# Norm rows spread through DRAM instead of TensorE transposes, and key blocks in plain order

## The chip, the cores and the metric

The kernel runs on one core of a Trainium2 chip. A core has TensorE (PE: matrix products into PSUM), VectorE (DVE), ScalarE (ACT), GpSimd (POOL), SyncE (SP, which here only issues DMAs) and 16 DMA engines. Each engine works through its own instructions in order and waits on semaphores for the others. The metric is the device time of one execution in microseconds; before the change the median of three runs is 2652.79 (2652.48 to 2655.35).

## What is computed

A trunk of two layers over 2048 tokens of 1024 channels, in fp32. Cut to what matters here:

```
# layer A
h    = rms_norm(x, a_norm)
u, z = split(h @ w_in)
x    = x + ((pool(u) @ w_group * scale) * silu(z)) @ w_out
x    = x + (p[0] @ ple_w[0]) * sigmoid(x @ ple_gate_w[0])
# shared keys and values, from the stream after layer A
k, v = split(rms_norm(x, kv_norm) @ w_kv);   k = rms_norm(per head of k, k_norm)
# layer B
q, z = split(rms_norm(x, b_norm) @ w_in);    q = rms_norm(per head of q, b_q_norm)
o    = stick_breaking_attention(q, k, v)     # strictly causal, 16 heads of 64
x    = x + (o * silu(z)) @ w_out
x    = x + (p[1] @ ple_w[1]) * sigmoid(x @ ple_gate_w[1])
```

`rms_norm` multiplies each token by one number, 1/sqrt(mean of its squares + eps), and each channel by a gain. The gains are folded into the weights. The token numbers are multiplied in after the product: `(x @ w)` of a token times that token's number.

## The kernel before

**Layout.** Activations lie channel by channel: a tile has 128 channels as partitions and 512 tokens along its free dimension. The 2048 tokens are four chunks (`s`) of 512. Every fp32 operand of a product is split into a high and a low part, and a product is three matmuls of 128x512 (high by high, high by low, low by high).

**The first part** (lines 212 to 885) is a list of 22 steps per chunk: for each group g in 3, 2, 1, 0 a gate product `run_z` and a `run_u`; four `run_o`; four `run_g`; then `run_kvq` twice each for q, k and v. A gate or u product is 48 matmuls of 512 columns (two outputs, eight `kt`, three matmuls). A `run_kvq` step has two halves, token pairs `j0` = 0 and 2, each 48 matmuls over eight weight units (`kt`, six matmuls per unit). The weights of a step are fetched two steps ahead and converted (split into parts, with the gain) one step ahead: for the wide weights of q, k and v the first four units at the start of the step before, the other four in its middle (`mid`, line 855). The conversion of q, k, v weights is L148 on ACT and L149 on VectorE. Weights that come back in later chunks are stored converted and only reread (`reread`, line 111).

**What orders the work.** `keep_in_program_order` pins an instruction to its place in its engine's order; the others are placed by the compiler's scheduler. DMAs go through `queue` (line 88), which issues on SyncE and pins them in this part. `pend` (line 86) is a list of stores that `stored_late` (line 95) issues at the third weight unit of the next product; `late` is a list of finishing pieces that `settle` (line 265) runs after the next gate product or v half.

**Token norms of layer A.** `prep(s)` makes the norms of the chunk's tokens, `r`, a tile of 128 x 4: token `j*128 + t` is at partition t, column j. Products lie with tokens along the free dimension, so `r` is needed as a row of 512 tokens, equal on all 128 partitions. `bcast` (line 237) does that: four TensorE transposes of `r[:, j]` spread over 128 columns (L241) into PSUM, and an ACT copy to `rb` (L246). It is called after the first gate product (g = 3) of a chunk (line 482; for chunk 0 later, in `run_u`). `gate_of` then multiplies the gate product by `rb` (L490), and `run_u` the u product (L508). PSUM for these products is six banks (four and two), two per product.

**Token norms of layer B.** In the first q step the norms after layer A, `r2s[s]`, are made in the same way, 128 x 4 (line 634). Here the tokens are in another order: token `4*t + j` is at partition t, column j. The gate branch of layer B, `gate_z(c)` (line 1060), runs beside the attention, for chunks 3, 2, 1, 0, piece by piece between the attention's own matmuls. It reads eight pairs `xz`, makes its own row `rb` with four transposes (L1069) into a bank that it borrows from the attention (`psar`, from `psl` at the start, from `psa` later, two banks each) and an ACT copy that orders the tokens (L1071), and multiplies each product by it (L1077).

**Keys.** `keyed` and `normed` take the products of q and k with tokens as partitions, evacuate them (`qs`, L721), make per-head norms (`sqq`, `ssq`, `rq`), multiply (L732) and transpose them in 32x32 blocks on VectorE (L734) into the tile `blocks`. For each of four 128-token tiles j the transpose writes every fourth element, so that `blocks` holds a head's tokens in the order (t j). When the fourth is written, `finish(m)` for four m goes to the list `lag`, which runs in the next step after its first 48 matmuls: a copy to the high part on ACT and a subtraction on VectorE for the low part (for k L743 and L744, 512 elements each; for q L747 and L748, with the gain), and a store to DRAM.

**The second part** (lines 888 to 1310) is the attention: 160 slots of one head, 512 queries and 512 keys, each with two score matmuls (L956, L957), a sigmoid (L960), a scan on VectorE (L968, L965), transposes (L981), a split (L984, L985) and two matmuls with the values (L993, L994). Between them go the pieces of the gate branch and of the output part (L1043, L1045, L1047), in shares worked out beforehand.

Of the kernel before, what the change touches and what calls it, by code (L numbers as in the profile page):

```python
# [9 lines left out]
F32 = mybir.dt.float32  # L10
F32R = mybir.dt.float32r
AF = mybir.ActivationFunctionType
ALU = mybir.AluOpType
AX = mybir.AxisListType

P = 128
D = 1024
S = 2048
KT = D // P
# [3 lines left out]
W5 = 512  # L23
NSUB = S // W5
# [6 lines left out]
def f(ap):  # L31
    return ap.bitcast(F32)
# [3 lines left out]
def trunk_kernel(ctx, tc, x, xt, pt0, wut, cols, heads, zin, grp, aout, agate, aple,  # L36
                 bq, kv, bz, bout, bgate, bple, outt):
    nc = tc.nc
# [28 lines left out]
    qd = [[[dram.tile([2, 4, P, P], F32, name=f"qd{i}{s}_{m}") for i in range(2)] for m in range(NH // 2)] for s in range(NSUB)]  # L67
    kd = [[dram.tile([2, 4, P, P], F32, name=f"kd{s}_{m}") for m in range(NH // 2)] for s in range(NSUB)]
    vd = [[dram.tile([8, W5, P], F32, name=f"vd{s}_{b}") for b in range(2)] for s in range(NSUB)]
    ve = [[dram.tile([4, W5], F32, name=f"ve{s}_{b}") for b in range(2)] for s in range(NSUB)]  # L70

    wod = [dram.tile([P, 2, 2, 4, P], F32, name=f"wod{o}") for o in range(KT)]
# [13 lines left out]
    pend = []  # L86
# [125 lines left out]
    with ExitStack() as st:  # L212
# [17 lines left out]
        hp = st.enter_context(tc.tile_pool(name="hp", bufs=1))  # L230
        work = hp.tile([P, 4, HALO + W5], F32, name="work")
        blocks = work.rearrange("q e n -> q (e n)")[:, 0 : 4 * W5].rearrange("q (g t j) -> q g t j", j=4, t=32)
        halo = [[hp.tile([P, HALO], F32, name=f"halo{o}_{i}") for i in range(2)] for o in range(KT)]
        for o in range(KT):
            V.memset(halo[o][0], 0.0)
# [231 lines left out]
        def run_z(s, g, wz):  # L467
            ck = chunk[s]
            beside = ()
            if not s and g == 3:  # L470
                beside = first_beside()
                wz = wz0["pair"]
            elif not s and g:
                beside = turning(g - 1)
            pss2 = [dense(), dense()]
            product(pss2, wz, ck["x"], (0, P), range(KT), beside)
            settle()
            if not s and g == 3:
                ck["z3"] = pss2
                return  # L480
            if "rb" not in ck:
                ck["rb"] = bcast(ck["r"], "x")
            gate_of(ck, g, pss2)

        def gate_of(ck, g, pss2):
# [122 lines left out]
        def run_kvq(s, kind, b, ws):  # L608
            ck = chunk[s]
            for j0 in (0, 2):  # L610
                if j0 and state["mid"]:
                    state.pop("mid")()
                    state["mid"] = None
                pss2 = [dense(), dense()]
                for kt in range(KT):
                    for i in range(2):
                        tk = slice((j0 + i) * P, (j0 + i + 1) * P)
                        for xh, wh in ((0, 0), (1, 0), (0, 1)):
                            T.matmul(pss2[i], ck["x2"][kt][:, xh, tk], wst(ws, kt, wh, 0, W5),  # L619
                                     start=(kt == 0 and xh == 0 and wh == 0), stop=(kt == KT - 1 and wh == 1))  # L620
                    if kt == 2:
                        stored_late()
                    while j0 == 0 and kt == KT - 1 and lag:
                        lag.pop(0)()
                    if kind != "q" and kt == 4 and s + 1 < NSUB:
                        next(ck["nxt"], None)
                if "r2" not in ck:
                    ps = turned()
                    for j in range(4):
                        T.matmul(ps[:, 0, j : j + 1], ck["acc"][:, j * P : (j + 1) * P], ones,  # L630
                                 start=True, stop=True)
                    ss = t2.tile([P, 4], F32, tag="ssx", name="ss2")
                    A.copy(out=ss, in_=ps[:, 0, 0:4])
                    rsqrt_mean(r2s[s], ss, D, t2, "x")
                    ck["r2"] = r2s[s]
                fins = [fin for i in range(2) for fin in token_major(s, kind, b, j0 + i, pss2[i])]
                if kind == "v":
                    settle()
                    (early["v"] if s == NSUB - 1 and b else late).extend(fins)
                else:  # L640
                    for fin in fins:
                        fin()
                quarter = {("q", 1): 0, ("k", 0): 1, ("k", 1): 2, ("v", 0): 3}.get((kind, b))
                if quarter is not None and j0 == 0 and s + 1 < NSUB:
                    load_x(s + 1, quarter)
                    load_tokens(s + 1, quarter)
                    if "nxt" not in ck:
                        ck["nxt"] = prep(s + 1)
            if kind == "v" and b == 1 and s + 1 < NSUB:
                for _ in ck["nxt"]:  # L650
                    pass
# [78 lines left out]
        def normed(s, kind, b, j, qs, rq):  # L730
            tc.keep_in_program_order(
                V.tensor_tensor(out=qs, in0=qs, in1=rq.unsqueeze(2).to_broadcast([P, 8, HD]), op=ALU.mult))  # L732
            tc.keep_in_program_order(
                V.transpose(out=blocks[:, :, :, j], in_=qs.rearrange("q h (g t) -> q (h g) t", t=32)))  # L734
            if j < 3:
                return

            def finish(m):
                hl = t2.tile([P, 2, 2, 2, P], F32R, tag="t4", name="hl", bufs=4)
                src = blocks[:, 4 * m : 4 * m + 4].rearrange("q (e g) t j -> q e g (t j)", e=2)  # L740
                hi, lo = hl[:, :, 0], hl[:, :, 1]
                if kind == "k":
                    A.copy(out=hi, in_=src)  # L743
                    V.tensor_tensor(out=lo, in0=src, in1=f(hi), op=ALU.subtract)  # L744
                else:
                    for g in range(2):
                        A.activation(out=hi[:, :, g], in_=src[:, :, g], func=AF.Identity, scale=gqk[:, g : g + 1])  # L747
                        V.scalar_tensor_tensor(out=lo[:, :, g], in0=src[:, :, g], scalar=gqk[:, g : g + 1],  # L748
                                               in1=f(hi[:, :, g]), op0=ALU.mult, op1=ALU.subtract)

                def store():
                    whole = f(hl).rearrange("q e l g n -> q e (l g n)")
                    if kind == "k":
                        queue(out=kd[s][4 * b + m].rearrange("e a (p x) n -> (a p) e (x n)", x=4), in_=whole)
                        return
                    qa, qb = qd[s][4 * b + m]
                    queue(out=qa.rearrange("e a (p x) n -> (a p) e (x n)", x=4), in_=whole)
                    for l in range(2):
                        queue(out=qb.rearrange("e a (p l g) n -> l (a p) e (g n)", l=2, g=2)[l],
                              in_=f(hl)[:, :, 1 - l].rearrange("q e g n -> q e (g n)"))  # L760

                pend.append(store)

            for m in range(4):
                lag.append(lambda m=m: finish(m))
# [122 lines left out]
    with ExitStack() as st:  # L888
# [171 lines left out]
        def gate_z(c):  # L1060

            xs = chunk[c]["x2"] if c == NSUB - 1 else []
            for o in range(len(xs), KT):
                pr = pair("xz")
                nc.sync.dma_start(out=f(pr), in_=x2p[c][o])
                xs.append(pr)
            ps = (psl if "w" in early else psa).tile([P, 4, P], F32, tag="psl" if "w" in early else "psa", name="psar")
            for j in range(4):
                T.transpose(ps[:, j, :], r2s[c][:, j : j + 1].to_broadcast([P, P]), ident)  # L1069
            rb = kap.tile([P, W5], F32, tag="rb", name="rb")  # L1070
            A.copy(out=rb.rearrange("q (t j) -> q t j", j=4), in_=ps.rearrange("q j t -> q t j"))  # L1071
            for o in range(KT):
                wz = early.pop("w") if "w" in early else stored(wzd[o])
                ps = dense()
                yield from piecewise(ps, wz, xs, 0)
                zr = t2.tile([P, W5], F32, tag="tmp", name="zr", bufs=4)
                V.tensor_tensor(out=zr.rearrange("q (t j) -> q t j", j=4), in0=ps.rearrange("q (j t) -> q t j", j=4),  # L1077
                                in1=rb.rearrange("q (t j) -> q t j", j=4), op=ALU.mult)

                def silu(o=o, zr=zr):  # L1080
                    sg = t2.tile([P, W5], F32, tag="tmp", name="sgz", bufs=4)
                    stay(A.activation(out=sg, in_=zr, func=AF.Sigmoid))  # L1082
                    G.tensor_tensor(out=zr, in0=zr, in1=sg, op=ALU.mult)  # L1083
                    nc.sync.dma_start(out=zd[c][o], in_=zr)

                soon(1, silu)
                if c == 0:
                    pair_up(NSUB - 1)
# [272 lines left out]
```

## Time and profile before

| what | value |
|---|---|
| median of three runs | 2652.79 us (2652.48 to 2655.35) |
| profiled execution | 2653.59 us, span of its instructions 2651.8 us |
| TensorE clock granted | 1.0 throughout |
| first part, until the last v product | to about 1305 us |
| VectorE busy in 1305 to 1720 us | 398.3 of 414.7 us |
| DMA | 600.40 MB, mean 226 GB/s |

A row of a timeline reads: start in us, duration in us, engine, source line, operation, tile written <- tiles read, partitions x elements, count of merged instructions, and in brackets the idle time of the engine before it and who ended that. `SPq` is SyncE's queue. A row by source line gives counts and the durations' minimum, median and maximum in ns. A row of waits gives who waited <- for whom, the total in us, the number of times and the longest. Of the chain of waits a row is start, duration, what. Matmuls overlap, so the duration of one (0.39 us) is longer than the distance from one to the next (0.227 us).

### The profile page before, as it was taken

The page shows a single profiled execution, that of the slowest core. Times are in us where ns is not written, and L with a number is a line of the kernel's source. Part 1 is how long each engine was busy: PE and PEld are TensorE (multiplying, and loading weights), DVE is VectorE, ACT ScalarE, POOL GpSimd, SP SyncE. Part 2 cuts the span into 40 slices and gives each one's busy share as a digit, 9 for nine tenths or more (in the row PEclk, how much of TensorE's full clock was granted, in tenths as well). Part 3 has the DMA queues.
Part 4 walks back from the last instruction along what each step waited for, and adds up shares of the span by engine and source line. Part 5 has one row for each costly group of instructions (what it writes and reads, how often), then busy time and mean ns, then how long its engine had stood idle before and what let it go on. Part 6 is the DMA issues. An engine that isn't in the chain of part 4 may idle for free.

```text
span 2651.8 us, 38568 instructions
## 1 busy us (share of the span) xinstructions
PE 2640.3 (100%) x13102; PEld 2205.3 (83%) x13102; DVE 1984.8 (75%) x2570; ACT 1427.5 (54%) x2767; POOL 939.8 (35%) x740
## 2 busy tenths in 40 slices
PE   9999999999999999999999999999999999999999
PEld 8888888888888888888888888888888888888887
DVE  6767835677367763767599999999999998886633
ACT  5446523556136641455466666666666666665531
POOL 2665437644485444753221111122111211212220
PEclk9999999999999999999999999999999999999999
DMA  8658885587856878447787665556766777779865
GB/s 325 227 165 302 283 314 186 191 300 253 308 177 225 301 237 304 147 153 240 229 277 229 187 215 170 175 164 194 209 200 173 190 217 238 201 209 287 248 229 178
DMA packets 469826, 600.40 MB, mean 226 GB/s; under 512 B 28607, under 2 KB 308415, under 8 KB 469629
## 3 DMA queue, kind: packets, MB, share of 16 engines
q1 hardware_dynamic: 463272, 587.39, 67.7%
q0 software_dynamic: 4608, 8.39, 2.0%
q10 hardware_dynamic: 1748, 2.17, 0.3%
q8 instruction: 103, 1.69, 0.3%
q14 instruction: 95, 0.77, 0.1%
HBM read 438.40 MB, written 153.16 MB: 223 GB/s over the span
## 4 chain that ended last, share of the span: by engine, by line
PE 89%; DMA 3%; DVE 2%; POOL 2%; ACT 2%; issue 1%; SPq 0%; ACTq 0%; DVEq 0%; POOLq 0%
PE psd L619 16%; PE psa L981 9%; PE psd L166 8%; PE psd L167 8%; PE psd L168 8%; PE psd L1043 6%; PE psd L1045 6%; PE psd L1047 6%; PE pso L994 5%; PE psl L957 5%; PE pso L993 5%; PE psl L956 5%; DMA wraw<-in_bq_dram 1%; PE psdt L1043 1%; PE psdt L1045 1%
## 5 line engine op out<-in xcount | busy, mean ns | idle before, releaser
L619 PE MATMUL psd<-wpair,x 128*128 128x512 f32 x2304 | 525.6, 390 | 1.4 <-DVE wpair L149 0.8
L968 DVE TENSOR_TENSOR_SCAN pp<-kap,pp,zeros 128x512 f32<-128x512 f32 x384 | 512.7, 1337 | 7.8 <-ACT kap L960 7.1
L984 ACT CAST at<-psa 128x512 fp32r<-128x512 f32 (+3 forms) x640 | 325.7, 523 | 348.8 <-PE psa L981 337.8
L619 PEld LDWEIGHTS psd<-wpair,x 128*128 128x128 f32 x2304 | 431.7, 188 | 93.0 <-DVE wpair L149 2.2
L985 DVE TENSOR_TENSOR at<-psa,at 128x512 fp32r<-128x512 f32 (+3 forms) x640 | 374.9, 598 | 62.2 <-ACT at L984 57.7
L960 ACT ACTIVATE kap<-psl 128x512 f32<-128x512 f32 (+3 forms) x640 | 345.7, 540 | 93.9 <-PE psl L957 90.4
L981 PE MATMUL psa<-ident,pp 128*128 128x128 f32 x2176 | 329.4, 273 | 2.3 <-DVE at L985 1.5
L981 PEld LDWEIGHTS psa<-ident,pp 128*128 128x128 f32 x2176 | 263.7, 141 | 58.4 <-DVE at L985 4.2
L956 PE MATMUL psl<-kk,qa 128*128 128x512 f32 (+3 forms) x640 | 275.1, 430 | 0.2 <-DMA kk<-kd 0.2
L965 DVE TENSOR_TENSOR_SCAN pp<-kap,ahead 128x128 f32<-128x128 f32 (+3 forms) x256 | 224.2, 877 | 40.2 <-ACT kap L960 38.8
L994 PE MATMUL pso<-at,vv 128*128 128x512 f32 (+3 forms) x640 | 234.0, 366 | 0.0
L957 PE MATMUL psl<-kk,qb 128*128 128x512 f32 (+3 forms) x640 | 232.9, 364 | 0.0
L993 PE MATMUL pso<-at,vv 128*128 128x512 f32 (+3 forms) x640 | 232.2, 363 | 0.0
L167 PE MATMUL psd<-xp,wpair 128*128 128x512 f32 x512 | 199.5, 390 | 1.4 <-DVE xp L320 1.4
L166 PE MATMUL psd<-xp,wpair 128*128 128x512 f32 x512 | 200.1, 391 | 0.7 <-ACT xp L319 0.7
L168 PE MATMUL psd<-xp,wpair 128*128 128x512 f32 x512 | 199.3, 390 | 0.0
L149 DVE SCALAR_TENSOR_TENSOR wpair<-wraw,gains,wpair 128x512 fp32r<-128x512 f32 x192 | 164.8, 891 | 31.9 <-ACT wpair L148 30.9
L143 POOL TENSOR_TENSOR wpair<-wraw,wpair 128x512 fp32r<-128x512 f32 x99 | 145.1, 1475 | 78.9 <-ACT wpair L141 72.2
L148 ACT ACTIVATE wpair<-wraw,gains 128x512 fp32r<-128x512 f32 x192 | 129.7, 716 | 47.4 <-DMA wraw<-in_bq_dram 35.6
L1083 POOL TENSOR_TENSOR zr<-zr,sgz 128x512 f32<-128x512 f32 x32 | 61.4, 1919 | 263.8 <-ACT sgz L1082 236.6
L141 ACT CAST wpair<-wraw 128x512 fp32r<-128x512 f32 x148 | 89.1, 618 | 104.5 <-PE psd L168 61.1
L994 PEld LDWEIGHTS pso<-at,vv 128*128 128x128 f32 x640 | 120.3, 188 | 26.4
(206 smaller groups left out, 5400.4 us busy)
## 6 DMA issues: line engine op xcount, KB each, us to landing
kk<-kd SPq DMA_DIRECT2D x160, 256.0 KB
vv<-vd SPq DMA_DIRECT2D x160, 256.0 KB
wraw<-in_kv_dram SPq DMA_DIRECT2D x128, 256.0 KB
wpair<-wzd SPq DMA_DIRECT2D x64, 512.0 KB
wpair<-wod SPq DMA_DIRECT2D x64, 512.0 KB
wpair<-wgd SPq DMA_DIRECT2D x64, 512.0 KB
wpair<-wu SPq DMA_DIRECT2D x48, 512.0 KB
wpair<-wi SPq DMA_DIRECT2D x36, 512.0 KB
```

The source lines that it names most:

```text
L166: T.matmul(ps, wst(units, kt, 0, c0), acts[kt][:, 0], start=(begin and kt == order[0]), stop=False)
L167: T.matmul(ps, wst(units, kt, 0, c0), acts[kt][:, 1], start=False, stop=False)
L168: T.matmul(ps, wst(units, kt, 1, c0), acts[kt][:, 0], start=False, stop=(end and kt == order[-1]))
L619: T.matmul(pss2[i], ck["x2"][kt][:, xh, tk], wst(ws, kt, wh, 0, W5), start=(kt == 0 and xh == 0 and wh == 0), stop=(kt == KT - 1 and wh == 1))
L956: T.matmul(ps[:, :w], qa[:, qs], kk[:, :w], start=True, stop=False)
L957: T.matmul(ps[:, :w], qb[:, qs], kk[:, :w], start=False, stop=True)
L960: A.activation(out=kp[:, r0:], in_=ps[:, :w], func=AF.Sigmoid, scale=-1.0)
L968: V.tensor_tensor_scan(out=pp[:, ::-1], data0=kp[:, ::-1], data1=zeros.to_broadcast([P, W5]), initial=st["carry"][j], op0=ALU.mult, op1=AL ...
L981: T.transpose(pt[:, j * P : (j + 1) * P], pp[:, r0 + kt * P : r0 + (kt + 1) * P], ident)
L985: V.tensor_tensor(out=at[:, 1, cs], in0=pt[:, cs], in1=f(at[:, 0, cs]), op=ALU.subtract)
L993: T.matmul(po[:, cs], vv[:, kt, :], at[:, 0, cs], start=(st["diag"] and kt == 0), stop=False)
L994: T.matmul(po[:, cs], vv[:, kt, :], at[:, 1, cs], start=False, stop=(st["last"] and kt == 3))
```

## The change

Three edits.

1. For chunks 1 to 3, `r` is no longer transposed. A store of `r` to a DRAM tile `rxd[s]` (token order, 512 pieces of four bytes) joins `pend` ahead of the first gate product, so it is issued at its third unit; at the seventh unit (`kt == 6`) a DMA reads the row back onto all 128 partitions (256 KB written). Both go through `queue`, pinned. Chunk 0 keeps `bcast`.
2. For the gate branch, `r2s[s]` is stored to `r2d[s]` through `pend` in the first q step, and `gate_z` reads it back by a DMA onto all partitions. Transposes, the borrowed bank and the ACT copy go, for all four chunks. `rb` there remains one buffer.
3. For keys the block transpose writes tokens in the order (j t), contiguous for each j; the finish reads them in the order (t j), in steps of 32 elements (128 bytes), and is cut in two pieces of 256 elements per m. Queries stay as they were.

```
+    rxd = [dram.tile([4, P], F32, name=f"rxd{s}") for s in range(NSUB)]
+    r2d = [dram.tile([P, 4], F32, name=f"r2d{s}") for s in range(NSUB)]
...
+        plain = work.rearrange("q e n -> q (e n)")[:, 0 : 4 * W5].rearrange("q (g j t) -> q g j t", j=4, t=32)
...
         def run_z(s, g, wz):
+            if s and g == 3:
+                pend.append(lambda: queue(out=rxd[s].rearrange("j t -> t j"), in_=ck["r"]))
+
+                def spread():
+                    ck["rb"] = t2.tile([P, W5], F32, tag="rb", name="rbx", bufs=1)
+                    queue(out=ck["rb"], in_=rxd[s].rearrange("j t -> (j t)").unsqueeze(0).to_broadcast([P, W5]))
+
+                def behind():
+                    for kt in range(KT):
+                        if kt == 6:
+                            spread()
+                        yield
+
+                beside = behind()
...
-            if "rb" not in ck:
-                ck["rb"] = bcast(ck["r"], "x")
             gate_of(ck, g, pss2)
...
                     ck["r2"] = r2s[s]
+                    pend.append(lambda: queue(out=r2d[s], in_=r2s[s]))
...
-                V.transpose(out=blocks[:, :, :, j], in_=qs.rearrange("q h (g t) -> q (h g) t", t=32)))
+                V.transpose(out=plain[:, :, j] if kind == "k" else blocks[:, :, :, j], in_=qs.rearrange("q h (g t) -> q (h g) t", t=32)))
...
                 if kind == "k":
-                    A.copy(out=hi, in_=src)
-                    V.tensor_tensor(out=lo, in0=src, in1=f(hi), op=ALU.subtract)
+                    at = plain[:, 4 * m : 4 * m + 4].rearrange("q (e g) j t -> q e g t j", e=2)
+                    for e in range(2):
+                        hi, lo = (hl[:, e, l].rearrange("q g (t j) -> q g t j", j=4) for l in range(2))
+                        A.copy(out=hi, in_=at[:, e])
+                        V.tensor_tensor(out=lo, in0=at[:, e], in1=f(hi), op=ALU.subtract)
...
-            ps = (psl if "w" in early else psa).tile([P, 4, P], F32, tag="psl" if "w" in early else "psa", name="psar")
-            for j in range(4):
-                T.transpose(ps[:, j, :], r2s[c][:, j : j + 1].to_broadcast([P, P]), ident)
             rb = kap.tile([P, W5], F32, tag="rb", name="rb")
-            A.copy(out=rb.rearrange("q (t j) -> q t j", j=4), in_=ps.rearrange("q j t -> q t j"))
+            nc.sync.dma_start(out=rb, in_=r2d[c].rearrange("t j -> (t j)").unsqueeze(0).to_broadcast([P, W5]))
```

## Prediction

> **What bounds the kernel now.** I read the page's totals first, then the waits of TensorE, the chain of waits, and the timelines of single stretches.
>
> ```profile
> span 2651.8 us, 38568 instructions
> PE 2640.3 (100%) x13102; PEld 2205.3 (83%) x13102; DVE 1984.8 (75%) x2570; ACT 1427.5 (54%) x2767; POOL 939.8 (35%) x740
> ...
> PE psd L619 <- DVE wpair L149: 0.8, 1, 0.8
> PE psa L981 <- ACT rb L1071: 0.7, 1, 0.7
> ...
> 232.91 120.25 PE psd L619 x528
> ...
> 550.33 119.80 PE psd L619 x528
> ```
>
> The span is TensorE: 2640.3 us busy of 2651.8. "Busy" alone would prove little, but the chain of waits shows 528 matmuls of 512 columns in 119.80 us, 0.227 each, without a hole. So time comes off only where TensorE loses work or one of its few waits, and goes on only where a new wait appears. Two waits lie at places the change touches: 0.8 us for converted weights (L149), 0.7 us for the spread norms of the gate branch (L1071). The profiled execution took 2653.59 us, 1.8 more than its span; the three timed runs have a median of 2652.79 (2652.48 to 2655.35). I work out differences on the span and add them to that median. What a measurement here can tell from no change is about 0.2%, 5.3 us.
>
> **The transposes that go.** Timeline of TensorE at the first gate product of chunk 1, and where the gate branch's second spread stands:
>
> ```profile
> 363.88 0.60 PE L241 MATMUL pst<-ident,rx 128*128 128x128 f32 x4
> 364.24 0.48 PE L166 MATMUL psd<-xp,wpair 128*128 128x512 f32 x1
> 364.55 0.39 PE L167 MATMUL psd<-xp,wpair 128*128 128x512 f32 x1
> ...
> 1422.22 0.40 PE L994 MATMUL pso<-at,vv 128*128 128x512 f32 x1
> 1423.30 0.66 PE L981 MATMUL psa<-ident,pp 128*128 128x128 f32 x4 [0.69 <-ACT rb L1071]
> ```
>
> From the start of the four transposes to the next matmul is 0.36 us, and that matmul takes 0.31 to the next instead of 0.227: 0.44 us per group. Chunks 1 to 3 lose one group each and the gate branch four: 7 x 0.44 = 3.1 us, all of it on the path, since nothing else ends last there. The gate branch's group also holds a bank of the attention's transposes until ACT has copied it: start to start is 1.08 us at 1422 instead of 0.23, so 0.85 more goes; with small remains elsewhere I take 1.0 (estimate). Together 4.1 us off. The ACT copies that go were off the path.
>
> **What takes their place on the queues.** Chunk 1, the SyncE queue and its neighbours, with the window from 364 to 375 us (last three columns: clock, DMA share, GB/s) and the nearest DMA whose landing is recorded; then the gate branch from chunk 3 to chunk 2:
>
> ```profile
> 333.82 1.01 POOL L81 TENSOR_TENSOR rx<-ms,neghalf 128x4 f32<-128x4 f32 x1
> ...
> 360.66 5.28 SPq L90 DMA_DIRECT2D wpair<-wi  x4
> 366.04 6.44 SPq L90 DMA_DIRECT2D vd<-vv  x3
> 372.57 3.29 SPq L90 DMA_DIRECT2D wpair<-wu  x4
> ...
> 374.75 1.37 DVE L508 TENSOR_TENSOR work<-psd,rbx 128x512 f32<-128x512 f32 x2 [8.32 <-PE psd L168]
> ...
> 364.00:375.00 11.00, 11.00 (x52) 9.15 (x51) 1.54 (x3) 1.81 (x3) 2.54 (x2) 1.00 1.03 375
> ...
> os<-ob POOLq DMA_DIRECT2D x16, 256.0 KB, 4.4
> ...
> 1421.63 0.65 DVE L1077 TENSOR_TENSOR zr<-psd,rb 128x512 f32<-128x512 f32 x1
> ...
> 1426.77 0.32 SPq L1084 DMA_DIRECT2D zd<-zr  x1
> ...
> 1442.79 0.67 DVE L1077 TENSOR_TENSOR zr<-psd,rb 128x512 f32<-128x512 f32 x1
> ```
>
> The norms are ready at 334.8 (rx), long before. The store is queued behind the wi loads and the vd stores behind the read, so SyncE issues the store at about 366, in the middle of a stretch where the DMA engines are full (share 1.03, 375 GB/s, so 512 KB take 1.4 us). The store waits out what is queued ahead, some four to six such transfers, 6 to 8 us. The read waits for the store's landing and needs a few us more: the nearest row is 4.4 us for 256 KB. That puts the norms at about 376 to 378, after the product's end at 363.9, not within it. VectorE waits for them in front of the gate's multiply; behind it on VectorE stand the u product's two L508, due at 374.75, which slip by some 3 us. TensorE does not feel it: a gate product's two PSUM banks are asked for again two products later, at about 386 (six banks, two per product, 10.9 us each). What SyncE delays is the three vd stores and then the weights of the product at 386. They were issued from 372.57; while the DMA engines still drain what is ahead, only the 3 us or so are lost in which they run dry. At most 8 transfers of 1.4 us ahead of them put them at 384 at the latest before, so 2 to 5 us of cover. I put this edit at nothing; if the cover went, each us beyond it would cost 1 us in each of three chunks.
>
> In the gate branch the read of the next chunk's row waits until the last multiply with the old one (1421.63 to 1422.28) is done. SyncE issued nothing until 1426.77, so the read fits in; by 4.4 us it lands near 1427, and the next multiply with it starts at 1442.79. Nothing, again. The token store of r2 is one small DMA behind stores that wait longer: nothing.
>
> **The keys' blocks.** This is the step that decides. What each operation costs now, by source line:
>
> ```profile
> L259 ACT CAST x<-tx x32: 1075/1108/1137, 180.8 to 1177.5; 128x512 fp32r<-128x512 f32 x32
> L260 DVE TENSOR_TENSOR x<-tx,x x32: 1073/1253/2103, 182.4 to 1178.6; 128x512 fp32r<-128x512 f32 x32
> L250 ACT CAST kpair<-kraw x40: 388/614/632, 143.9 to 1157.0; 128x512 fp32r<-128x512 f32 x32, 128x256 fp32r<-128x256 f32 x8
> L743 ACT CAST hl<-work x32: 613/617/623, 305.3 to 1276.5; 128x512 fp32r<-128x512 f32 x32
> L246 ACT COPY rbx<-pst x4: 587/587/587, 43.5 to 999.9; 128x512 f32<-128x512 f32 x4
> L1071 ACT COPY rb<-psar x4: 586/586/589, 1306.3 to 1717.2; 128x512 f32<-128x512 f32 x4
> L744 DVE TENSOR_TENSOR hl<-work,hl x32: 670/684/694, 305.9 to 1277.4; 128x512 fp32r<-128x512 f32 x32
> L734 DVE STREAM_TRANSPOSE work<-qs x64: 1080/1094/1122, 240.6 to 1273.8; 128x512 f32<-128x512 f32 x64
> ```
>
> The transpose now writes every fourth element, 1094 ns; contiguous, no row shows it. Its bounds are 684 (L744, 512 contiguous elements on the same engine) and 1094; I take 684, because L260 reads at the same 16-byte steps and takes 1073 at best. So 0.41 us less for each of 32. In return the finish reads steps of 128 bytes, in pieces of 256 elements, twice as many. A contiguous piece of 256 takes 388 ns on ACT (L250's least). For the step the nearest row is L259: reading at 16-byte steps takes 1108 against 617, 0.49 more for 512 elements, 0.245 for 256. So 388 to 635 ns; I take 635, because L259's step also leaves its neighbours behind each time. Between two in a row ACT overlaps 0.1 us: 0.53 each. VectorE's subtractions grow alike (L744's 684 towards L260's 1073 for 512 elements, in halves), beside ACT's casts and no later than they.
>
> [...]
>
> Now where this stands. The last transposes of one k step and the finish come just ahead of the conversions that the next step needs:
>
> ```profile
> 304.14 1.10 DVE L734 STREAM_TRANSPOSE work<-qs 128x512 f32<-128x512 f32 x1
> ...
> 305.27 1.67 ACT L743 CAST hl<-work 128x512 fp32r<-128x512 f32 x3 [9.50 <-DVE work L734]
> 306.85 0.61 ACT L319 CAST xp<-xin 128x512 fp32r<-128x512 f32 x1
> 307.37 0.61 ACT L743 CAST hl<-work 128x512 fp32r<-128x512 f32 x1
> 307.89 0.68 ACT L721 ACTIVATE qs<-psd,r2all 128x512 f32<-128x512 f32 x1
> ...
> 315.93 1.78 DVE L149 SCALAR_TENSOR_TENSOR wpair<-wraw,gains,wpair 128x512 fp32r<-128x512 f32 x1
> ...
> 335.24 4.43 DVE L149 SCALAR_TENSOR_TENSOR wpair<-wraw,gains,wpair 128x512 fp32r<-128x512 f32 x4 [1.63 <-ACT wpair L148]
> ...
> 632.28 0.75 DVE L149 SCALAR_TENSOR_TENSOR wpair<-wraw,gains,wpair 128x512 fp32r<-128x512 f32 x1
> ...
> 633.88 2.66 DVE L149 SCALAR_TENSOR_TENSOR wpair<-wraw,gains,wpair 128x512 fp32r<-128x512 f32 x4
> ...
> 951.85 14.53 PE L619 MATMUL psd<-wpair,x 128*128 128x512 f32 x62 [0.83 <-DVE wpair L149]
> ```
>
> ACT stands still 9.5 us for the transpose, then does the finish, and only then evacuates the next keys (qs), whose squares, norm and multiply stand ahead of the L149 conversions on VectorE. So ACT's finish shifts the whole chain: four casts at 0.52 become eight at 0.53, +2.2, and the transpose ends 0.41 earlier: +1.75 us. How much cover is there? The first v step begins seven half steps of 10.89 after the rows above: at 309.1 in chunk 0 and 626.6 in chunk 1. Its unit 6 is first needed 38 matmuls later (0.227 each), at 317.7 and 635.2, and is ready at 317.71 and about 634.55 (first of the four at 633.88); unit 5 in chunk 1 at 633.0 for 633.8. So the cover is nothing in chunk 0, 0.6 in chunk 1, and in chunk 2 TensorE waits already (0.83 at 951.85). Chunk 3 has no next chunk to prepare beside it; I put it at nothing. That makes 1.7 + 1.15 + 1.75 = 4.6 us. The second v step meets the next finish, with the first delay still in the chain: in chunk 0 its first late unit is ready not before 336 for 337, so some 0.9 us there, 0.5 in chunk 1, none in chunk 2, whose TensorE is itself later: 1.4 us. In all 6.0 us, with bounds of 0 (388 ns pieces) and well above.
>
> **Sum:** 4.1 off, 6.0 on: +1.9 us on the median, 2654.7.
>
> **The rivals.** *The steps cost ACT nothing.* Eight at 0.30 are 2.4 for 2.1, and the transpose pays that back: no new wait, -4.1, and with the 0.8 that TensorE waits today -4.9: 2647.9. For it: reads from PSUM in large steps are not dearer here (L1071 takes 586 ns as L246 takes 587). Against it: L259, L260 and L734, all in SBUF.
>
> *The 128-byte step costs more than the 16-byte one.* Slower, at the same place: each 0.1 us on a piece adds 0.8 us to the chain in three chunks, and again in the second v step. At 0.75 per piece the chain is 3.5 late: 3.45 + 2.9 + 3.5 in the first v steps and about 5.7 in the second, 15.5; less 4.1 is +11.4, 2664.2. It decides from about 0.62 per piece, where the sum passes 5.3. For it: nothing in the trace is as far apart; the cover is nil. Against it: each step leaves its neighbours already at 16 bytes.
>
> *The store is slow.* 512 pieces of four bytes may take far longer than the queue ahead. From some 4 us over my 6 to 8, weights come late in three chunks; 4 us beyond that cover gives +12 and 2667. For it: no row has such a store. Against: it moves 2 KB. [...]
>
> *It isn't what it says:* attention may be paced by VectorE, so that the gate branch's transposes give nothing: +1.8 worse, 2656.5, inside the forecast's own range. Against it: one matmul follows the other there too.
>
> **How the numbers follow.** Forecast 0.55 (2651 to 2658), no cost of steps 0.20, dearer steps 0.19, slow store 0.06. Faster by over 5.3 us needs the whole first rival and a little luck: 0.08 of its 0.20, and 0.02 from elsewhere, 0.10. Slower: most of the dearer steps (0.16), of the slow store (0.05) and 0.04 of the forecast's upper end, 0.25. Same: 0.65. The range reaches from 2647.2, just beyond the first rival's time, to 2661.0, into the dearer steps at about 0.68 per piece; it leaves out 0.06 below and 0.14 above.
>
> **What would show it.** Right: TensorE has 28 matmuls fewer; waits of TensorE for L149 grow to about 6 us in chunks 0 to 2, none in chunk 3; the finish's casts take about 635 ns and the keys' transposes about 684; VectorE's first gate multiply in chunks 1 to 3 starts some 11 us later without a wait of TensorE. Wrong: casts near 388 ns, transposes still at 1094, or TensorE waiting for weights in the gate products or for rb in attention.

## The result, and the profile after

The changed kernel takes 2673.14 us (median of six runs, 2671.99 to 2675.75); the kernel before took 2654.17 in six runs beside it (2652.48 to 2655.35). The ratio is 1.0074 (95% interval 1.0061 to 1.0087): slower by some 19 us. The forecast was 2654.7 with a range up to 2661.0; the measured time lies beyond it. The profiled execution took 2673.71 us; its span is 20.0 us longer than before.

The totals on the page of the profile, as quoted of before:

```profile
span 2671.8 us, 38591 instructions
...
PE 2644.3 (99%) x13074; PEld 2207.6 (83%) x13074; DVE 1993.2 (75%) x2602; ACT 1445.3 (54%) x2792; POOL 939.4 (35%) x740
```

TensorE has the 28 instructions fewer, and is yet busy 4.0 us longer; the other 16 us are waits. TensorE's waits (who <- for whom, total, times, longest):

```profile
PE psd L168 <- DMA wpair<-wu: 10.6, 3, 4.0
PE psd L634 <- DVE wpair L151: 6.2, 4, 2.3
...
PE pst L645 <- POOL acc L619: 0.6, 1, 0.6
```

The second row is the keys' edit: the converted weights that cost 0.8 us before (L149 there, L151 here). The first is new: three times, once in each of chunks 1 to 3, the second u product of the chunk waits for its weights from DRAM. SyncE's queue in chunk 1 shows why:

```profile
363.68 4.53 SPq L92 DMA_DIRECT2D wpair<-wi  x3
368.30 0.39 SPq L92 DMA_DIRECT2D rxd<-rx  x1
379.82 0.32 SPq L92 DMA_DIRECT2D rbx<-rxd  x1
380.23 4.14 SPq L92 DMA_DIRECT2D vd<-vv  x3
384.46 2.68 SPq L92 DMA_DIRECT2D wpair<-wu  x1
```

Store issued at 368.30, read issued at 379.82, when the store had landed: 11.5 us in which SyncE issues nothing. The windows of the same stretch (the last two columns are DMA share and GB/s) show the DMA engines running dry:

```profile
372.00:374.00 2.00, 2.00 (x10) 1.66 (x9) 0.00 (x0) 0.00 (x0) 0.00 (x0) 1.00 0.96 349
374.00:376.00 2.00, 2.00 (x11) 1.65 (x10) 0.00 (x0) 0.00 (x0) 0.00 (x0) 1.00 0.07 11
376.00:378.00 2.00, 2.00 (x11) 1.65 (x10) 0.00 (x0) 0.00 (x0) 0.00 (x0) 1.00 0.00 0
...
380.00:382.00 2.00, 2.00 (x10) 1.66 (x9) 0.00 (x0) 0.00 (x0) 0.00 (x0) 1.00 0.00 0
382.00:384.00 2.00, 2.00 (x10) 1.68 (x9) 0.00 (x0) 0.00 (x0) 0.00 (x0) 1.00 0.85 190
```

The queue ahead is done by about 374.6, and then nothing moves for 7 us. The weights behind are issued 11.9 us later than before (384.46 against 372.57). VectorE's first gate multiply, and then TensorE at the second u product:

```profile
384.49 0.69 DVE L505 TENSOR_TENSOR zr<-psd,rbx 128x512 f32<-128x512 f32 x1 [20.21 <-DMA rbx<-rxd]
...
387.90 0.39 PE L170 MATMUL psd<-xp,wpair 128*128 128x512 f32 x1
391.64 0.75 PE L168 MATMUL psd<-xp,wpair 128*128 128x512 f32 x1 [3.36 <-DMA wpair<-wu]
392.19 0.63 PE L169 MATMUL psd<-xp,wpair 128*128 128x512 f32 x1
392.62 0.63 PE L170 MATMUL psd<-xp,wpair 128*128 128x512 f32 x1
```

Besides the wait there is a second cost: behind it the matmuls start 0.43 us apart in place of 0.227. The windows on either side (after PEld, DVE, ACT, POOL comes the granted clock):

```profile
384.83:388.25 3.42, 3.42 (x16) 2.52 (x14) 3.42 (x5) 1.27 (x2) 2.30 (x3) 1.00 1.13 330
388.25:391.66 3.41, 0.05 (x2) 0.05 (x1) 0.60 (x2) 0.00 (x0) 3.41 (x5) 1.00 1.00 370
391.66:395.07 3.41, 3.41 (x8) 2.76 (x9) 2.21 (x4) 0.62 (x1) 1.98 (x4) 0.50 1.03 418
395.07:398.48 3.41, 3.41 (x16) 2.79 (x16) 2.44 (x3) 0.00 (x0) 2.15 (x2) 1.00 1.02 413
```

For 3.41 us the granted clock is 0.50: 8 matmuls instead of 16, 1.7 us lost. This happens five times in after, never before: behind the three waits for wu and behind the two longest waits of the keys (at 320.0 and 968.5 us). In two of the five windows TensorE stands for a part, and less is lost: it is busy 3.41, 3.41, 2.91, 3.13 and 3.41 us in them, 16.3 in all, and half of that is the loss.

The ledger on the span: transposes and the borrowed bank 4.1 off (forecast); waits for wu 10.6 on; waits for converted weights 6.2 less 0.8, 5.4 on; half clock 8.1 on; GpSimd's `acc` 0.6 on. That is 20.6 against 20.0 measured.

### The profile page after: what moved, and what is told of

Same layout as the page of the kernel before. It is cut to its first block, busy times and chain, and to the rows that moved or that the text cites. A ratio compares the mean times of both kernels' runs of the same rounds, so it can differ in the third digit from the quotient of the medians.

```text
span 2671.8 us, 38591 instructions
## 1 busy us (share of the span) xinstructions
PE 2644.3 (99%) x13074; PEld 2207.6 (83%) x13074; DVE 1993.2 (75%) x2602; ACT 1445.3 (54%) x2792; POOL 939.4 (35%) x740
## 4 chain that ended last, share of the span: by engine, by line
PE 81%; POOL 5%; DMA 4%; DVE 4%; ACT 3%; issue 3%; SPq 0%; ACTq 0%; DVEq 0%; POOLq 0%
PE psa L1000 9%; PE psd L634 8%; PE psd L168 8%; PE psd L169 7%; PE psd L170 7%; PE psd L1062 6%; PE psd L1064 6%; PE psd L1066 6%; PE pso L1013 5%; PE psl L976 5%; PE pso L1012 5%; PE psl L975 5%; POOL rq L83 2%; DVE wpair L151 1%; DMA wraw<-in_bq_dram 1%
## 5 line engine op out<-in xcount | busy, mean ns | idle before, releaser
L168 PE MATMUL psd<-xp,wpair 128*128 128x512 f32 x512 | 201.8, 395 | 11.8 <-DMA wpair<-wu 10.6
L151 DVE SCALAR_TENSOR_TENSOR wpair<-wraw,gains,wpair 128x512 fp32r<-128x512 f32 x192 | 166.1, 897 | 33.3 <-ACT wpair L150 33.3
```

The lines of the kernel that those rows point to most:

```text
L168: T.matmul(ps, wst(units, kt, 0, c0), acts[kt][:, 0], start=(begin and kt == order[0]), stop=False)
```

## The experiments

The theory after this reading: edit 1 costs the time, because its store of 512 four-byte pieces lands late and SyncE stands at the read with the weights behind it; edit 3 costs about what was forecast; edit 2 gains. The rival: it is the edits together, the row's wait biting only on a chain that the keys' blocks have made longer. All ratios are to the kernel before, timed beside it on the same chip.

### Each edit alone

**`only_row`: edit 1 alone.**

```
+            if s and g == 3:
+                pend.append(lambda: queue(out=rxd[s].rearrange("j t -> t j"), in_=ck["r"]))
...
-            if "rb" not in ck:
-                ck["rb"] = bcast(ck["r"], "x")
```

> Only the first edit: the row of layer A's norms stored at the third unit of the first gate product and read back at the seventh; gate branch and keys as before. Theory (the store's landing holds SyncE, so the weights of the third product after it come late, and TensorE then runs some us at half clock): SyncE waits about 11 us between store and read in chunks 1 to 3, TensorE waits 3 to 4 us for weights there, each followed by 3.4 us at clock 0.5; about 16 us on, 1.3 us off for the transposes, so 2669 us. Rival (the late weights need the delays of the keys' edit as well): TensorE waits under 1 us there, the time within 3 us of before.

Measured: 2669.73 us, ratio 1.0066 (1.0053 to 1.0080). TensorE's waits, with two others left out between:

```profile
PE psd L167 <- DMA wpair<-wu: 7.8, 2, 4.3
PE psd L167 <- DVE work L528: 4.9, 1, 4.9
```

Three waits again, in the second u product of the three chunks (the view names a VectorE result at one of them), 12.7 us, with half clock behind each: for 3.4 us in chunk 1 and for 6.8 in chunks 2 and 3. TensorE was busy 13.1 us in these stretches, so some 6.5 us are lost. Store to read takes 11.6 to 12.9 us. The loss needs no other edit: the rival falls.

**`only_gate`: edit 2 alone.**

```
+                    pend.append(lambda: queue(out=r2d[s], in_=r2s[s]))
...
-            for j in range(4):
-                T.transpose(ps[:, j, :], r2s[c][:, j : j + 1].to_broadcast([P, P]), ident)
...
+            nc.sync.dma_start(out=rb, in_=r2d[c].rearrange("t j -> (t j)").unsqueeze(0).to_broadcast([P, W5]))
```

> Only the second edit: the gate branch of layer B reads its row of norms back from DRAM; layer A's row and the keys as before. Theory (TensorE paces the attention, transposes and the borrowed bank are all that changes): 16 matmuls fewer, the 0.7 us wait of TensorE for the spread row gone, no wait of VectorE for the row over 1 us; 1.8 + 1.2 us off, about 2651 us. Rival (VectorE paces the attention): within 0.5 us of before. Second rival (SyncE, held by the read until the last multiply with the old row, brings keys or weights late): slower by 1 us or more, with TensorE waiting for a DMA.

Measured: 2649.11 us, ratio 0.9986 (0.9978 to 0.9995), 3.5 us off (1.3 to 5.8); the prediction's share for this edit was 4 x 0.44 + 1.0 = 2.8. No wait for `rb` appears in the attention, and none for the row's DMA on TensorE.

**`only_plain`: edit 3 alone.**

```
-                    A.copy(out=hi, in_=src)
...
+                    at = plain[:, 4 * m : 4 * m + 4].rearrange("q (e g) j t -> q e g t j", e=2)
+                    for e in range(2):
...
+                        A.copy(out=hi, in_=at[:, e])
```

> Only the third edit: keys transposed contiguously, finish in two pieces with 128-byte steps. Theory (the finish's casts sit ahead of the next keys' evacuation on ACT, with no cover before the first v step's late weight units): casts at about 670 ns, transposes at about 700, TensorE waits for converted weights 2.2 us in chunks 0 and 2, 1.2 in chunk 1, none in chunk 3, and the two waits of over 2 us are each followed by 3.4 us at clock 0.5; 7 to 9 us on, about 2662 us. Rival (these waits in the changed kernel came from the row's store instead): no new wait for converted weights, 0 to 1 us off.

Measured: 2660.80 us, ratio 1.0032 (1.0020 to 1.0044), 8.5 us on (5.3 to 11.7). Waits:

```profile
PE psd L620 <- DVE wpair L149: 6.2, 5, 2.2
PE pst L631 <- POOL acc L605: 1.7, 1, 1.7
```

The same 6.2 us as in after, plus one late GpSimd sum. There is no half clock in this profile, though two were expected and one wait is 2.2 us long; the last section shows where that wait fell.

By the medians the three edits alone come to 17.1 on, 3.5 off and 8.2 on, 21.8 in all; together they cost 19.0. So the edits do not make each other dearer.

### Is it the waiting, the queue ahead, or the pieces?

**`row_early`: edits 1 and 2, the store issued as soon as the norms are made** (in the last v step), eight weight loads ahead of the read, so that the landing should be over when SyncE comes to the read.

```
                 chunk[s]["r"] = r
+                if s:
+                    queue(out=rxd[s].rearrange("j t -> t j"), in_=r)
...
-                pend.append(lambda: queue(out=rxd[s].rearrange("j t -> t j"), in_=ck["r"]))
```

> First and second edit, keys as before, and the store of layer A's row moved ahead on SyncE: issued where the norms are made, in the last v step, eight weight loads ahead of the read instead of just ahead of it. Theory (only SyncE's wait for the store's landing costs): no wait of SyncE over 2 us between them, TensorE without waits in the gate and u products, clock 1.0; 28 transposes and one bank wait off, 4 us off, about 2650 us. Rival (the 256 KB that the read moves in a stretch with full DMA engines, or VectorE's late multiply, brings the waits): TensorE still waits 2 us or more per chunk and the time is above before.

Measured: 2661.76 us, ratio 1.0035 (1.0022 to 1.0049), 12.7 us above `only_gate`. The expectation failed. SyncE and the DMA windows:

```profile
351.17 2.27 SPq L92 DMA_DIRECT2D rxd<-rx  x1
356.65 0.36 SPq L92 DMA_DIRECT2D vd<-vv  x1
357.10 9.01 SPq L92 DMA_DIRECT2D wpair<-wu  x4
```

```profile
359.00:361.00 2.00, 2.00 (x10) 1.65 (x9) 0.69 (x1) 0.02 (x1) 0.00 (x0) 1.00 0.58 20
```

SyncE does not stand at the read here, and the weights are late all the same (TensorE waits for wu three times, 8.7 us in all, and loses 3.1 more in two half clocks): behind the small pieces the transfers run at 20 GB/s. The rival's cause, the 256 KB of the read, does not fit: the read is issued at 372.19, when TensorE's wait in chunk 1 is over (367.75). So my theory of the wait was only half of it; the next four runs separate the parts.

**`store_only`: the kernel before plus the store alone**, read by nobody.

```
+            if s and g == 3:
+                pend.append(lambda: queue(out=rxd[s].rearrange("j t -> t j"), in_=ck["r"]))
```

> The kernel before with one addition: layer A's token norms are stored as 512 pieces of 4 bytes in chunks 1 to 3, as the change does, but nobody reads the row back; the norms are still spread by TensorE. Theory (SyncE stands at the read's issue until the store has landed, and the weights are queued behind it): without the read nobody waits for the landing, so no new wait of TensorE for wu, and a time within 1.5 us of the kernel before, 2652 to 2654 us. Rival (the 4-byte pieces themselves hold up every transfer behind them on the rings, whether or not SyncE waits): the rings are silent for some 5 us behind the pieces here too, and what is queued behind them lands some 5 us later; the waits for wu come back in part, 2655 to 2662 us.

Measured: 2655.33 us, ratio 1.0008 (0.9998 to 1.0017): by its time no more than a small cost, but the rival is seen in the trace. DMA rates in chunk 1 behind the pieces, which move at 370.4 to 371.1:

```profile
372.00:374.00 2.00, 2.00 (x11) 1.65 (x10) 0.05 (x1) 0.00 (x0) 0.00 (x0) 1.00 1.26 36
376.00:378.00 2.00, 2.00 (x10) 1.67 (x9) 0.00 (x0) 0.00 (x0) 1.98 (x3) 1.00 1.04 25
380.00:382.00 2.00, 2.00 (x11) 1.65 (x10) 0.96 (x2) 0.63 (x1) 1.56 (x3) 1.00 0.92 156
```

From 372 to 378 us what is queued behind the pieces crawls at 23 to 36 GB/s, with the DMA engines recorded as busy (shares of 1.04 to 1.34); at 382 the rate is back (360). In chunks 2 and 3 it falls to 9 and 10 GB/s (692 to 694 and 1011 to 1013 us). TensorE's waits at the second u product:

```profile
PE psd L167 <- DMA wpair<-wu: 2.1, 2, 1.4
PE psd L167 <- DVE zr L493: 1.6, 1, 1.6
```

That is one wait in each of the three chunks, 3.7 us (the view names a VectorE result at the first). The weights are not later because SyncE, which waits for no landing here, issues the first of them at 371.86, in after at 384.46. At this place in the queue the pieces alone cost 1.7 us (0.5 off to 4.5 on) and edit 1 as a whole 17.1: most of the loss needs SyncE to stand at the read until they have landed.

**`store_apart`: the same store, each four-byte piece 512 bytes from the next.**

```
-    rxd = [dram.tile([4, P], F32, name=f"rxd{s}") for s in range(NSUB)]
+    rxd = [dram.tile([4, P, 128], F32, name=f"rxd{s}") for s in range(NSUB)]
...
-                pend.append(lambda: queue(out=rxd[s].rearrange("j t -> t j"), in_=ck["r"]))
+                pend.append(lambda: queue(out=rxd[s].rearrange("j t u -> t j u")[:, :, 0:1], in_=ck["r"].unsqueeze(2)))
```

> The store alone again, 512 pieces of 4 bytes that nobody reads, but each piece goes to an address of its own 512 bytes from the next, in place of side by side in one row. With the pieces side by side the transfers behind them pause for some 5 us. If pieces in the same stretch of memory wait for each other, the pause shrinks under 2 us here; if it is the count of pieces (or their size below some unit), it stays at 4 to 6 us. Either way the time is within 3 us of the kernel before.

Measured: 2652.15 us, ratio 0.9998 (0.9988 to 1.0008), no wait for wu, and in the same windows:

```profile
372.00:374.00 2.00, 2.00 (x10) 1.66 (x9) 0.00 (x0) 0.00 (x0) 0.00 (x0) 1.00 1.15 347
376.00:378.00 2.00, 2.00 (x11) 1.65 (x10) 0.25 (x1) 0.00 (x0) 1.97 (x4) 1.00 1.15 350
380.00:382.00 2.00, 2.00 (x11) 1.65 (x10) 1.27 (x2) 0.62 (x1) 1.25 (x1) 1.00 1.02 406
```

In the windows named of chunks 2 and 3 it is 411 and 289 GB/s. As many pieces of the same size, and no pause at all. So neither the count nor the size of the pieces makes the pause by itself: the two runs differ only in how the pieces lie, side by side in 2 KB of DRAM in `store_only` (23 to 36 GB/s from 372 to 378 us), 512 bytes apart here. Whether a row stored apart would also land early for its read was not tried.

**`row16`: edit 1 alone, the row token-major, 128 pieces of 16 bytes**; the two multiplies read it in steps.

```
-    rxd = [dram.tile([4, P], F32, name=f"rxd{s}") for s in range(NSUB)]
+    rxd = [dram.tile([P, 4], F32, name=f"rxd{s}") for s in range(NSUB)]
...
-                pend.append(lambda: queue(out=rxd[s].rearrange("j t -> t j"), in_=ck["r"]))
+                pend.append(lambda: queue(out=rxd[s], in_=ck["r"]))
...
-                V.tensor_tensor(out=zr, in0=pss2[k], in1=ck["rb"], op=ALU.mult)
+                V.tensor_tensor(out=fours(zr), in0=fours(pss2[k]), in1=by_token(ck), op=ALU.mult)
```

> Edit 1 alone, but the row lies in DRAM as [128, 4], token-major, so that the store is 128 pieces of 16 bytes in place of 512 of 4, and the two multiplies read the row through a strided view. The gate branch's store of 128 pieces of 16 bytes is followed by about 2 us of silent rings in the profile of after, the 4-byte one by about 5. Theory (the landing is late by the queue ahead and by the many small pieces): store to read falls from 11.5 to about 8 us, TensorE's waits for wu from 5.0, 3.6 and 4.5 to 1.5, 0 and 1 us, no half clock behind them, so 2654 to 2658 us. Rival (the queue ahead of the store alone makes it late): store to read stays at 11 to 12 us, 2668 to 2670 us. The strided view may add some tenths of a us to each multiply of the attention phase.

Measured: 2651.26 us, ratio 0.9991 (0.9982 to 1.0001), 18.5 us under `only_row` (19.5 with each taken against the kernel before beside it). SyncE in chunk 1:

```profile
363.76 0.38 SPq L91 DMA_DIRECT2D rxd<-rx  x1
370.78 0.32 SPq L91 DMA_DIRECT2D rbx<-rxd  x1
371.19 3.48 SPq L91 DMA_DIRECT2D vd<-vv  x3
374.76 3.43 SPq L91 DMA_DIRECT2D wpair<-wu  x4
```

Store to read takes 7.0 us (6.7 in the other two chunks), just what the prediction gave to the queue ahead, and TensorE waits for wu no more, nor is there a half clock. It came out below the 2654 to 2658 expected, since I had left some waits standing. The queue ahead lies within the cover; the pieces' landing was the whole cost. The multiplies take longer through the view (a mean of 0.97 us against 0.68), beside TensorE.

**`act_store`: edit 1 alone, the store on ScalarE's own DMA queue.**

```
-  pend.append(lambda: queue(out=rxd[s].rearrange("j t -> t j"), in_=ck["r"]))
+  pend.append(lambda: tc.keep_in_program_order(nc.scalar.dma_start(out=rxd[s].rearrange("j t -> t j"), in_=ck["r"])))
```

> Edit 1 alone with the store issued by ScalarE on its own DMA queue, so that nothing of SyncE's queue lies ahead of it; the read stays on SyncE. Theory: of the 11.5 us between store and read the 6 us of queue ahead go and the 5 us of the small pieces stay, so the store lands 5 to 7 us after its issue, SyncE stands less, and TensorE's waits for wu shrink to under 1 us each: 2653 to 2657 us. Rival (the small pieces are the whole cost): store to read stays above 10 us, 2667 to 2670 us.

Measured: 2679.14 us, ratio 1.0097 (1.0082 to 1.0112). The expectation failed, and in the other direction:

```profile
PE psd L167 <- DMA wpair<-wu: 21.2, 3, 7.2
```

ScalarE issues the store at 355.61, among the last v stores; what SyncE has issued then crawls at 20 to 40 GB/s from 359 to 367, and the u weights needed first are among it. Half clock follows each wait, some 5.3 us more (mean granted clock 0.996). A queue of its own did not help here: what lay on SyncE's queue crawled as well. That fits `row_early`, where nearly the same place on SyncE's queue cost 12.7 us.

### Is it the steps or the number of pieces?

**`halves`: the kernel before, the keys' finish cut into two contiguous pieces of 256.**

```
-                    A.copy(out=hi, in_=src)
-                    V.tensor_tensor(out=lo, in0=src, in1=f(hi), op=ALU.subtract)
+                    for e in range(2):
+                        A.copy(out=hi[:, e], in_=src[:, e])
+                        V.tensor_tensor(out=lo[:, e], in0=src[:, e], in1=f(hi[:, e]), op=ALU.subtract)
```

> The kernel before with the keys' finish cut into two pieces of 256 contiguous elements on ScalarE and on VectorE, in place of one of 512; the transposes are as before. It tells the count of pieces from their stride. Theory (the step of 128 bytes makes ScalarE's piece 0.67 us, so its chain of 16 pieces is what the first v step waits for): contiguous pieces take under 0.45 us, the chain grows by under 1 us and no wait comes up, within 1.5 us of the kernel before, 2652 to 2654 us. Rival (the doubled number of pieces and of semaphores is the cost, whatever the stride): the waits of 1.1 to 2.4 us at the first v step come up here too, 2658 to 2662 us.

Measured: 2653.77 us, ratio 1.0004 (0.9995 to 1.0013); the profiled execution is the slowest of ten, 2657.86. The piece, by source line (min/median/max ns), against those of after (one k step, chunk 0):

```profile
L744 ACT CAST hl<-work x64: 400/404/409, 306.7 to 1282.4; 128x256 fp32r<-128x256 f32 x64
```

```profile
L750 DVE STREAM_TRANSPOSE work<-qs x4: 703/709/712, 289.6 to 303.1; 128x512 f32<-128x512 f32 x4
L762 ACT CAST hl<-work x4: 662/670/675, 303.9 to 305.6; 128x256 fp32r<-128x256 f32 x4
```

Contiguous 404 ns, in steps of 128 bytes 670: the 0.27 us per piece are the steps', and twice the pieces without steps cost nothing that shows (0.1 us on the medians, with an interval up to 3.4 on).

### Putting it together

**`full_row16`: the changed kernel, all three edits, with the 16-byte row**, altered as in `row16`.

> The changed kernel, all three edits, with one thing altered: layer A's row is stored token-major, as 128 pieces of 16 bytes in place of 512 of 4. Theory (the small pieces of that store are what the prediction left out, and its other terms hold): the waits for wu and the half clock behind them go, the keys' waits of some 6 us at the first v steps stay, and the time falls from 2673 to 2654 to 2658 us, the prediction's own sum. Rival (part of the loss comes from the edits together, the row's wait falling on a chain that the keys' blocks have made longer): more than 2662 us.

Measured: 2656.76 us, ratio 1.0014 (1.0005 to 1.0023), 16.4 us under the changed kernel (4.0 on against the kernel before beside it, where the changed kernel has 19.0), within 2.1 of the forecast of 2654.7. The waits that are left:

```profile
PE psd L637 <- DVE wpair L151: 6.2, 4, 2.3
```

With them come two half clocks (319.9 and 958.2 us), 3.4 us. The sum 4.1 off, 5.4 on, 3.4 on gives +4.7; measured are +4.0 on the medians. The rival, that edits 1 and 3 make each other dearer, falls here too.

**`gate_row16`: edits 1 and 2, 16-byte row, keys as before.**

> Edits 1 and 2 without the keys' blocks, the row of layer A as 128 pieces of 16 bytes. Theory (the gains of the two rows add, and no wait stays): layer A's row at 16 bytes gave 2.4 us off, the gate branch's 3.5 off, so 2646 to 2649 us, faster than both kernels. Rival (the two rows' gains overlap, or the second store's place brings a wait): 2650 us or more.

Measured: 2648.29 us, ratio 0.9984 (0.9975 to 0.9992): no new wait, no half clock. It beats the kernel before by 4.5 us (2.1 to 6.6) and the changed one by far; from `only_gate` the measurement does not tell it apart, and the two gains alone (2.4 and 3.5) add up to 5.9, within the interval.

**`gate_row16_early`: the same with the store at the place of `row_early`.**

> As edits 1 and 2 with 16-byte pieces, but the store is issued as soon as the norms are made, among the last v step's stores, eight weight loads ahead of the read. With 4-byte pieces this place cost 12 us more than the gate row alone. Theory (the 4-byte pieces hold up the 512-byte stores and the weight loads around them, and 16-byte pieces do not): no wait of TensorE for wu, 2646 to 2650 us. Rival (a store of any piece size in that place holds the queue up): waits of 1 to 5 us for wu in chunks 1 to 3, 2655 us or more.

Measured: 2648.34 us, ratio 0.9984 (0.9975 to 0.9993), no wait for wu. The place that cost 12.7 us with four-byte pieces costs nothing with 16-byte ones.

## Why the prediction was wrong

**What bounds the kernel: right.** Of the 20.0 us all but a little stands in TensorE's waits and clock; no other engine's load shows in it.

**The transposes: right.** 28 instructions fewer, the bank wait gone, and for the gate branch 3.5 us measured against 2.8.

**Layer A's row: this is the step that failed.** It put the edit "at nothing", with the store landing 6 to 8 us after its issue, norms at 376 to 378, and 2 to 5 us of cover for the weights. Measured: 11.5 us from store to read; the first multiply at 384.49, not 376 to 378; the weights' issue 11.9 us later, of which 2.3 are the chunk's own delay (the queue reaches the row's place at 368.30 against 366.04), so 9.6. TensorE waits 3.5 of them (the mean of three): the cover was some 6 us, more than I took, but the delay was three times what I took. The size of the queue ahead was right (`row16`: 7.0 us, no wait); the term left out is the landing of 512 pieces side by side: the transfers ahead are done at about 374.6 and the read goes out 5.2 us later, in `row16` within 0.8 us (done by 370.0, read at 370.78). The rival "the store is slow" held this mechanism, at +12 us and a chance of 0.06. Its price was near for the waits (10.6); its chance, which no row of before gave, was too low. "It moves 2 KB" is an argument from bytes, and no row of before held a store of such pieces, so nothing in the trace spoke for the fast case either: an operation that no row shows should have had its slow end inside the range.

**The gate branch's row: right**, no cost. Its store goes in 16-byte pieces; behind three of them in after the DMA rate falls below 100 GB/s for 2 to 3 us (239 to 241, 564 to 567, 890 to 892 us), and in `only_gate` TensorE waits for no DMA.

**The keys' blocks: right in mechanism and nearly in size.** Transposes 709 ns (684 taken), pieces 670 (635), first v steps 2.1, 1.0 and 2.3 us, the last with the 0.8 of before in it (1.7, 1.15 and 2.6 forecast), the second v step only once, 0.7 (1.4 forecast in all): 5.4 us of new waits against 6.0. The prediction's 0.53, and the 0.62 to 0.75 of its dearer rival, are distances from the start of one piece to the next; measured are 0.57 (six pieces in 3.52 us in chunk 0), so that rival stays out. 128-byte steps cost 0.27 us per 256 elements (670 ns in after, 404 in `halves`), 16-byte steps by L259 of before 0.245.

**Not foreseen: the half clock.** No term had it. It adds 8.1 us to after, 4.9 behind the weights and 3.3 behind the keys' waits.

**The sum** therefore missed by 10.6 + 4.9 from the row and 3.3 at the keys; with the row mended alone it holds to 2.1 us. That this is so near is in part luck: 3.4 us there are half clock, which the sum did not have, and the other terms came out 1.3 lower than forecast.

## What to carry to other kernels

Before a row goes through DRAM, look at the pieces of its store and where they lie: four-byte pieces side by side held up everything behind them for about 10 us (`store_only`, below full rate from 372 to 382 us), 16-byte pieces for about 2 (`row16` moves nothing from 370 to 372 us), and moving the store earlier or to another queue only chose other victims (`row_early` 12.7 us above `only_gate`, `act_store` 2679.14 us). A DMA that must wait for a landing should be costed by what is queued behind it, and an operation that no row of the trace shows should keep its slow end inside the range. A new wait on TensorE can cost again in clock: in after each of five waits of 2.1 to 4.0 us was followed by 3.41 us at 0.50, up to 1.7 us lost each; in `only_plain` one of 2.2 us was not.

## What the runs showed of the hardware

**The half clock came on a fixed grid.** Within each run all changes of the granted clock lie multiples of 3.413 us apart; in after the half clock starts at 320.0, 391.7, 715.9, 968.5 and 1043.6 us and lasts 3.413 us each time. What went with it was TensorE's busy share in the 3.413 us before, in after 0.37, 0.01, 0.21, 0.41 and 0.05. In the 14 profiles, from 30 to 2550 us, all 19 windows of this grid with a share up to 0.42 were followed by one at half clock; none lies between 0.42 and 0.52, and of those above only two were, one that itself ran at half clock (0.65) and one in `halves` at 554.1 us (0.73), which stays unexplained. So the length of a wait is not enough. In `only_plain` a wait of 2.2 us fell across two windows:

```profile
955.99:959.40 3.41, 1.78 (x8) 1.13 (x6) 2.50 (x3) 3.38 (x6) 2.71 (x2) 1.00 0.00 0
959.40:962.82 3.42, 2.85 (x12) 2.36 (x13) 3.42 (x6) 2.85 (x5) 0.00 (x0) 1.00 0.48 152
```

Shares of 0.52 and 0.83 and the clock stayed at 1.00; in after a wait of 2.1 us inside one window (share 0.37) and one of 2.3 us (share 0.41) were each followed by half clock.

**Small writes side by side.** 512 pieces of four bytes into 2 KB (`store_only`): 23 to 36 GB/s for 6 us behind them and the full rate (360) again after some 10; the same pieces 512 bytes apart (`store_apart`): 347 to 406 in the windows shown. Why the two differ, and at what distance the pause ends, was not tried.
